# Two places in a planned attention phase: when head outputs are added up, and where memory rows' squares are written

## The chip, the cores and the metric

The kernel runs on one core of one Trainium2 chip. The metric is the device time of one execution in microseconds, as the median of several runs. A profile of one execution stands beside it, taken by the hardware profiler. The engines are called TensorE (PE; its weight loads PEld), VectorE (DVE), ScalarE (ACT), GpSimd (POOL) and SyncE (SP); SP does no arithmetic here and issues most of the transfers.

## The reference

One layer of a hybrid encoder, in f32, with 1024 positions and a width of 1024:

```python
h = rmsnorm(x, g_mix_pre)
proj = h @ w_in                       # q, k, v of 8 "fox" heads and of 8 "chunk" heads, head size 64
y_fox = forgetting_attention(...)     # causal, with a cumulative log forget-gate bias
y_chk = chunked_relpos_attention(...) # own chunk and 8 before it, with a relative-position bias
y = concat([rmsnorm(y_fox, g_fox_out), rmsnorm(y_chk, g_chk_out)])
x = x + rmsnorm(y @ w_out, g_mix_post)
h = rmsnorm(x, g_mem_pre)
mem_n = rmsnorm(mem, g_mem_kv)        # 256 memory rows
x = x + rmsnorm(memory_cross_attention(h, mem_n, w_mq, w_mk, w_mv, w_mo), g_mem_post)
h = rmsnorm(x, g_ff_pre)
x = x + rmsnorm(square(relu(h @ w_ff1)) @ w_ff2, g_ff_post)
```

## The kernel before

All matmuls keep f32 accuracy by splitting an operand into a high part, rounded to the matmul type, and a low part that holds the rest; a product is then three matmuls (high by high, low by high, high by low: lines 174 to 176).

The program has three phases: the input projection with both attentions, the output projection and the memory attention, and the feed-forward layer. The first two are laid out by a small planner, `Flow`. It keeps a clock of its own (`flow.now`). Several streams of steps for TensorE (scores, transposes of probabilities, products with v, projections as filler, and others) are offered in an order of preference; the first whose conditions hold is taken, and the clock moves on by the step's listed cost. Everything for VectorE, ScalarE, POOL and SP (named V, S, G and D) is listed with `flow.put(engine, at, cost, call, then, level)`: from `at` on it may be taken by its engine, a lower level goes first. So the listed times decide only the order in which each engine gets its instructions. On the chip each engine works through its own list in that order, and waits at an instruction until what it reads is there and the buffer that it writes is free.

`Tokens` stand for buffers: a step or a load takes tokens and later gives them back at a listed time, and `ready(n)` asks whether n are free. The buffers themselves come from pools: "u4" (line 155) has 31 buffers of 4 KB for each partition and is used for almost everything that lives long; "wraw" has three buffers for raw weights as they are loaded; "ph" (line 582) has two, in which the transposed probabilities, high and low part, wait for their product with v. The tokens of the "ph" buffers are `free["p"]`.

How one head's probabilities go: scores on TensorE (lines 515 and 516), bias and row minimum on VectorE (519), exponential on ScalarE (528), the reciprocal of the sum on VectorE (530), scaling on POOL (531), transposes on TensorE into `ptr` (588), high part on ScalarE (597), low part on VectorE (594), the product `pv` on TensorE (638), its copy `ot` on ScalarE (647), and two stores to DRAM on SP (654 and 656).

The product leaves a head output in three parts (high and low part of v by the high part of p, and high by low). They are stored into the three planes of `od[kc][th]`, where `kc` is one of the 8 blocks of 128 output columns (0 to 3 fox, 4 to 7 chunk) and `th` one of the two halves of the positions. When the eight stores of a block and half are through, `summed` (606) lists two transfers on POOL's queue that add plane 1 and then plane 2 onto plane 0 in DRAM (line 611). Both write the same rows, so the second waits until the first has landed. Only when all four blocks of a group are added may `Outputs` read them back.

`Stock` loads the weights through the "wraw" buffers in the order of a list. In this list "norm" stands ahead of the weights of the sixth pair of heads: there `mem_norm` takes all three raw buffers for the gain and for the two blocks of memory rows, squares the rows on ScalarE (line 831; only the sum along each row is used, the squares themselves go to a tile `junkm` that nobody reads), works out the inverse root on POOL, scales the rows on VectorE and stores them to DRAM on SP. "mem", further down the list, loads them back. `WeightSums` (910) adds up blocks of the memory output weights ahead of time and starts a set when eight "u4" tokens are free.

Of the kernel before, what the change touches and what calls it, by code (L numbers as in the profile page):

```python
# [14 lines left out]
F32 = mybir.dt.float32  # L15
F32R = mybir.dt.float32r
BF16 = mybir.dt.bfloat16
AF = mybir.ActivationFunctionType
# [4 lines left out]
P = 128  # L23
S = 1024
D = 1024
# [110 lines left out]
def build(ctx, tc, nc, out, t):  # L136
    def pool(name, bufs=1, space=None, stack=ctx, **kw):
        if space is not None:
            kw["space"] = space
        return stack.enter_context(tc.tile_pool(name=name, bufs=bufs, reuse_waits="tile", **kw))  # L140
# [12 lines left out]
    def u4(name, shape, dt=F32R):  # L153

        return up.tile(list(shape), dt, tag="u4", bufs=31, name=name)
# [56 lines left out]
    md = [dr.tile([P, D], F32, name=f"md{b}") for b in range(2)]  # L212
# [4 lines left out]
    p1 = pool("p1", stack=p1s)  # L217
# [8 lines left out]
    def bias_rows(part):  # L226

        if part == 0:
# [12 lines left out]
    flow = Flow()  # L241
    free = {k: Tokens(flow, n) for k, n in
            dict(s=2, tr=2, pv=2, mm=2, sp=5, p=2, klo=4, bias=2, raw=2, w=2, ot=3, qn=2, u4=7,
                 q=4, mp=4, pt=1, xt=2, wq=0).items()}
    seen = {}

    def there(*keys):
        return all(flow.past(seen.get(k, math.inf)) for k in keys)
# [4 lines left out]
    def raw_tile(name):  # L253
        return wp.tile([P, D], F32, tag="wraw", bufs=3, name=name)
# [7 lines left out]
    class Stock:  # L262
# [88 lines left out]
        def pump(self):  # L351

            while self.to_load:
                if isinstance(self.to_load[0], str):
                    n = 3 if self.to_load[0] == "norm" else 2
                    if not free["raw"].ready(n):
                        break
                    for _ in range(n):
                        free["raw"].take()
                    (mem_norm if self.to_load.pop(0) == "norm" else mem_loads)()  # L360
                    break
                key = self.to_load[0][0]
                self.spare[key] = not free["raw"].ready()
                if self.spare[key] and not (key[0] in SPARE and free["u4"].ready(12)):
                    break
                free["u4" if self.spare[key] else "raw"].take()
                self.load()
                flow.put("D", flow.now, 0.55, lambda: None, lambda at, k=key: seen.__setitem__(("raw", k), at + 4.2))
            while self.to_split and there(("raw", self.to_split[0])):
                key = self.to_split[0]  # L370
                home = self.home.get(key, "w")
                n = 1 + (home == "u4")
                if not free[home].ready(n):
                    break
                for _ in range(n):
                    free[home].take()
                self.to_split.pop(0)
                vec = key[0] not in "qkv" and (key[0] != "mk" or key[1] % 2)
                self.turned += 1

                def halves(at, key=key, eng="V" if vec else "G"):
                    e = nc.vector if eng == "V" else nc.gpsimd
                    last = lambda end: (seen.__setitem__(key, end), free["u4" if self.spare.get(key) else "raw"].give(end))
                    if eng == "V":
                        flow.put(eng, at, 1.22, lambda: self.lo(key, e), last, 1)
                    else:
                        flow.put(eng, at, 1.3, lambda: self.lo(key, e, 0), lambda end: flow.put(
                            eng, end, 1.3, lambda: self.lo(key, e, 1), last, 2), 2)

                flow.put("S", flow.now, 1.06, lambda key=key: self.hi(key), halves, 2)  # L390
# [212 lines left out]
    def value_steps():  # L603
        landed = [[all_of(("od", g, th), 4) for th in range(2)] for g in range(2)]

        def summed(kc, th):
            def add(at, m=1):
                if m == 3:
                    return landed[kc // 4][th](at)
                o = od[kc][th]  # L610
                flow.put("G", at, 0.9, lambda: nc.gpsimd.dma_start(o[0], o[m], accum_op=ALU.add, max_dma_last_dim=2048),
                         lambda end: add(end + 6.0, m + 1), 1)
            return all_of(("ot", kc, th), 8, add)

        sums = {(kc, th): summed(kc, th) for kc in range(KC) for th in range(2)}
        for n, a, g in units:
            kind, pr = ORDER[n]
# [50 lines left out]
    def all_of(key, m, then=None):  # L668

        count = [m, 0.0]  # L670

        def one(at):
            count[0] -= 1
            count[1] = max(count[1], at)
            if count[0] == 0:
                seen[key] = count[1]
                if then:
                    then(count[1])
        return one
# [139 lines left out]

    def mem_norm():  # L820

        g = raw_tile("g_mem_kv")
        nc.sync.dma_start(g, t["g_mem_kv"].to_broadcast([P, D]))
        for b in range(2):
            xt = raw_tile(f"mem{b}")
            nc.sync.dma_start(xt, t["mem"][b * P:(b + 1) * P, :])
            r, ss = (small.tile([P, 1], F32, tag=k, bufs=8, name=f"{k}_mem{b}") for k in ("rstd", "ss"))

            def square(xt=xt, ss=ss, b=b):
                junk = p1.tile([P, D], BF16, tag="ph", bufs=2, name=f"junkm{b}")  # L830
                nc.scalar.activation(junk, xt, AF.Square, scale=1.0 / 32.0, accum_out=ss)

            def root(r=r, ss=ss):
                nc.gpsimd.tensor_scalar(r, ss, EPS, None, op0=ALU.add)
                nc.gpsimd.tensor_tensor(r, r, mhalf[:, 0:1], op=ALU.pow)

            scale = lambda xt=xt, r=r: nc.vector.scalar_tensor_tensor(xt, xt, r, g, op0=ALU.mult, op1=ALU.mult)
            store = lambda xt=xt, b=b: nc.sync.dma_start(md[b], xt)
            flow.chain(flow.now + 6 + b, [("S", 1.1, square), ("G", 2.0, root), ("V", 1.3, scale), ("D", 0.55, store)],
                       lambda at, b=b: [free["raw"].give(at) for _ in range(1 + b)] and seen.__setitem__(("md", b), at))  # L840

    mem_in = []

# [673 lines left out]
    with tc.manual_schedule():  # L1517
# [96 lines left out]
        def value_banks(g, th):  # L1614
            tags = (("mm", "s"), ("tr", "pv"))[g]
            n = 264 if g == 0 else 256
            return [mm_tile([P, n], f"v{g}{th}{b}", tags[b // 2]) for b in range(4)]
# [25 lines left out]
        V = value_banks(0, 0)  # L1643
# [28 lines left out]
        V = value_banks(0, 1)  # L1672
# [38 lines left out]
    y, ss = ys["m", 1]  # L1711
# [220 lines left out]
    add = {}  # L1932
# [163 lines left out]
    with manual:  # L2096
        sums = lambda: None
        for j in range(NP):
# [10 lines left out]
            if j < AHEAD:  # L2109
                p1, g11 = saved.pop(j)  # L2110
                x = bank(f"px{j}")
            else:
                x, _, g11, add = first_row(j, w["a"])
# [250 lines left out]
```

## Time and profile before

| | us |
|---|---|
| median of 3 runs (lowest, highest) | 1458.66 (1458.56, 1458.72) |
| the profiled execution | 1458.23 |
| its span, from the first to the last instruction | 1456.4 |
| granted TensorE clock, mean | 0.999 of full speed |
| busy in the span: TensorE, VectorE, ScalarE, POOL | 1443.7, 955.3, 810.0, 409.2 |

In a row of the timeline the columns are start, duration, engine, line, operation, output and inputs, shapes, how many, and in brackets the idle time of the engine before it, with what ended it. A row of the chain has start, duration, and the engine and line that the chain goes through. "128x512" and the like are partitions by elements. Matmuls overlap: the next begins before the modelled end of the one before.

### The profile page before, as it was taken

What the parts mean: (1) busy time and instruction counts of PE and PEld (TensorE: products, weight loads), DVE (VectorE), ACT (ScalarE), POOL (GpSimd) and SP (SyncE); (2) the same over time, 40 slices, a digit from 0 to 9 for tenths busy, and PEclk for the clock granted to TensorE, in tenths of its full rate; (3) what the DMA queues carried; (4) which work ended last, traced back from release to release, by engine and by line L of the source; (5) the groups of instructions that cost most, each with busy time, mean ns of one, the idle gap of its engine ahead of it and who ended that gap; (6) DMA issues with size and microseconds to landing.
All of it is one profiled execution on the core that took longest, in us unless ns stands there. A gap on an engine that the chain in (4) does not pass through costs nothing.

```text
span 1456.4 us, 20947 instructions
## 1 busy us (share of the span) xinstructions
PE 1443.7 (99%) x7252; PEld 1221.4 (84%) x7252; DVE 955.3 (66%) x1647; ACT 810.0 (56%) x1435; POOL 409.2 (28%) x488
## 2 busy tenths in 40 slices
PE   9999999999999999999999999999999999999998
PEld 9988888788889888888888888888888888888886
DVE  4577777767667636965784697665555656655576
ACT  7457776567577654555654455545555453444442
POOL 1345566354344202421041514343331000000021
PEclk9999999999999999999999999999999999999999
DMA  8233566945538676541460646754444775345565
GB/s 334 67 100 98 139 170 173 294 111 127 135 91 250 186 230 238 176 172 59 140 222 30 211 147 235 261 195 159 159 158 160 289 311 190 136 149 190 187 246 202
DMA packets 100826, 259.44 MB, mean 178 GB/s; under 512 B 12504, under 2 KB 24928, under 8 KB 100720
## 3 DMA queue, kind: packets, MB, share of 16 engines
q1 hardware_dynamic: 95968, 249.71, 50.5%
q0 software_dynamic: 4608, 8.39, 4.0%
q8 instruction: 57, 0.93, 0.3%
q14 instruction: 49, 0.40, 0.1%
q10 hardware_dynamic: 144, 0.00, 0.0%
HBM read 181.98 MB, written 76.08 MB: 177 GB/s over the span
## 4 chain that ended last, share of the span: by engine, by line
PE 96%; DMA 1%; ACT 1%; DVE 1%; issue 0%; POOL 0%; SPq 0%; DVEq 0%; POOLq 0%; ACTq 0%
PE pv L638 4%; PE fx L175 4%; PE fx L174 4%; PE fx L176 4%; PE ptr L588 4%; PE px L176 3%; PE fy L174 3%; PE px L175 3%; PE fy L175 3%; PE px L174 3%; PE fy L176 3%; PE mq L174 2%; PE mq L176 2%; PE pz L176 2%; PE pz L175 2%; PE mq L175 2%
## 5 line engine op out<-in xcount | busy, mean ns | idle before, releaser
L594 DVE TENSOR_TENSOR p<-ptr,p 128x512 fp32r<-128x512 f32 (+1 forms) x152 | 92.2, 616 | 31.7 <-ACT p L597 30.9
L2087 ACT ACTIVATE whif<-ra 128x1024 fp32r<-128x1024 f32 x37 | 39.3, 1062 | 125.3 <-PE fy L175 62.6
L2089 DVE TENSOR_TENSOR wlof<-ra,whif 128x1024 fp32r<-128x1024 f32 x37 | 45.3, 1225 | 87.9 <-ACT whif L2087 87.9
L597 ACT ACTIVATE p<-ptr 128x512 fp32r<-128x512 f32 (+1 forms) x152 | 79.7, 538 | 38.8 <-PE ptr L588 38.2
L2201 POOL TENSOR_SCALAR rf<-sf 128x1 f32<-128x1 f32 x8 | 8.2, 1030 | 325.0 <-ACT jf L2186 324.7
L638 PE MATMUL pv<-p,vs 128*128 128x512 f32 (+1 forms) x304 | 86.5, 373 | 0.9 <-DVE p L594 0.9
L176 PE MATMUL fx<-vhif,wlof 128*128 128x512 f32 x168 | 65.4, 389 | 0.0
L174 PE MATMUL fx<-vhif,whif 128*128 128x512 f32 x168 | 65.4, 389 | 0.0
L175 PE MATMUL fx<-vlof,whif 128*128 128x512 f32 x168 | 65.4, 389 | 0.0
L1976 POOL TENSOR_TENSOR sc<-wf,wf 128x512 f32<-128x512 f32 x14 | 22.6, 1614 | 142.2 <-DMA wf<-in_w_ff 117.8
L638 PEld LDWEIGHTS pv<-p,vs 128*128 128x128 f32 x304 | 53.5, 189 | 10.2 <-DVE p L594 1.5
L174 PE MATMUL k<-hT_hi,whik 128*128 128x512 f32 x128 | 52.6, 411 | 0.0
L174 PE MATMUL mq<-h2T_hi,whimq 128*128 128x512 f32 x128 | 51.6, 403 | 0.2 <-DVE ym L1372 0.2
L647 ACT ACTIVATE ot<-pv 128x512 f32<-128x512 f32 x64 | 37.9, 593 | 24.9 <-PE pv L638 24.6
L174 PE MATMUL q<-hT_hi,whiq 128*128 128x512 f32 x128 | 51.0, 398 | 0.0
L174 PE MATMUL yw<-whiwo,yT_hi 128*128 128x512 f32 x128 | 50.8, 396 | 0.1
L175 PE MATMUL k<-hT_lo,whik 128*128 128x512 f32 x128 | 50.2, 392 | 0.0
L176 PE MATMUL k<-hT_hi,wlok 128*128 128x512 f32 x128 | 50.2, 392 | 0.0
L176 PE MATMUL q<-hT_hi,wloq 128*128 128x512 f32 x128 | 50.1, 391 | 0.0
L175 PE MATMUL q<-hT_lo,whiq 128*128 128x512 f32 x128 | 50.1, 391 | 0.0
L176 PE MATMUL mq<-h2T_hi,wlomq 128*128 128x512 f32 x128 | 50.0, 391 | 0.0
L175 PE MATMUL mq<-h2T_lo,whimq 128*128 128x512 f32 x128 | 50.0, 391 | 0.0
(670 smaller groups left out, 4953.8 us busy)
## 6 DMA issues: line engine op xcount, KB each, us to landing
ra<-gd SPq DMA_DIRECT2D x56, 512.0 KB, 3.5
wg<-in_w_ff SPq DMA_DIRECT2D x56, 512.0 KB, 4.5
wf<-in_w_ff SPq DMA_DIRECT2D x38, 512.0 KB, 3.7
gd<-s SPq DMA_DIRECT2D x48, 256.0 KB, 2.1
od<-ot SPq DMA_DIRECT2D x64, 128.0 KB, 3.1
od<-od POOLq DMA_DIRECT2D x32, 256.0 KB, 4.9
wrawmq<-in_w_mq SPq DMA_DIRECT2D x16, 512.0 KB, 4.4
gd<-u SPq DMA_DIRECT2D x32, 256.0 KB, 2.0
```

The costliest lines, as they stand in the source:

```text
L174: nc.tensor.matmul(ps, lh, rh, start=start, stop=False, skip_group_check=more)
L175: nc.tensor.matmul(ps, lh, rl, start=False, stop=False, skip_group_check=more)
L176: nc.tensor.matmul(ps, ll, rh, start=False, stop=stop, skip_group_check=more)
L588: nc.tensor.transpose(tr[:, m, :], sp[:, k * P:(k + 1) * P], ident)
L594: flow.put("V", at, 0.56 if dead else 0.7, lambda: nc.vector.tensor_sub(pl[:, live, :], tr[:, live, :], f(ph[:, live, :])), done)
L597: flow.put("S", flow.end, 0.49 if dead else 0.6, lambda ph=ph, tr=tr, live=live: nc.scalar.activation(ph[:, live, :], tr[:, live, :], AF.C ...
L638: nc.tensor.matmul(pv[:, :, q0 * P:(q0 + k1 - k0) * P], v, x[:, :, k0:k1, :].rearrange("p m k q -> p m (k q)"), start=c == 0 and m == 0, s ...
L647: nc.scalar.activation(box["t"][:, :, :, ::step], pv.rearrange("p m (k q) -> p m k q", q=P), AF.Copy)
L1976: eng.tensor_sub(sc[:, k1], r0[:, k0], r1[:, k0])
L2087: nc.scalar.activation(ah, ra, AF.Copy)
L2089: nc.vector.tensor_sub(al, ra, f(ah))
L2201: nc.gpsimd.tensor_scalar(r, ssf[b][:, 0:1], ssf[b][:, 1:2], EPS, op0=ALU.add, op1=ALU.add)
```

## The change

The two adding transfers of a block are listed later for the blocks 0 to 5: the first 3 us further behind the stores, and the next step 9 us instead of 6 us behind the end of each. Blocks 6 and 7 stay as they were. The squares of the memory rows go into a "u4" buffer, as f32, instead of a "ph" buffer, as bf16. For that `mem_norm` starts only when two "u4" tokens are free and takes both; each is given back when its square is through. The squares are listed 8 and 9 us after the loads instead of 6 and 7, and the rest of each row's chain follows its square as before.

```diff
--- before.py
+++ after.py
@@ -353,7 +353,7 @@
             while self.to_load:
                 if isinstance(self.to_load[0], str):
                     n = 3 if self.to_load[0] == "norm" else 2
-                    if not free["raw"].ready(n):
+                    if not free["raw"].ready(n) or n == 3 and not free["u4"].ready(2):
                         break
                     for _ in range(n):
                         free["raw"].take()
@@ -609,8 +609,8 @@
                     return landed[kc // 4][th](at)
                 o = od[kc][th]
                 flow.put("G", at, 0.9, lambda: nc.gpsimd.dma_start(o[0], o[m], accum_op=ALU.add, max_dma_last_dim=2048),
-                         lambda end: add(end + 6.0, m + 1), 1)
-            return all_of(("ot", kc, th), 8, add)
+                         lambda end: add(end + (6.0 if kc > 5 else 9.0), m + 1), 1)
+            return all_of(("ot", kc, th), 8, lambda at: add(at + (0.0 if kc > 5 else 3.0)))
 
         sums = {(kc, th): summed(kc, th) for kc in range(KC) for th in range(2)}
         for n, a, g in units:
@@ -819,6 +819,8 @@
 
     def mem_norm():
 
+        for _ in range(2):
+            free["u4"].take()
         g = raw_tile("g_mem_kv")
         nc.sync.dma_start(g, t["g_mem_kv"].to_broadcast([P, D]))
         for b in range(2):
@@ -827,8 +829,7 @@
             r, ss = (small.tile([P, 1], F32, tag=k, bufs=8, name=f"{k}_mem{b}") for k in ("rstd", "ss"))
 
             def square(xt=xt, ss=ss, b=b):
-                junk = p1.tile([P, D], BF16, tag="ph", bufs=2, name=f"junkm{b}")
-                nc.scalar.activation(junk, xt, AF.Square, scale=1.0 / 32.0, accum_out=ss)
+                nc.scalar.activation(u4(f"junkm{b}", (P, D), F32), xt, AF.Square, scale=1.0 / 32.0, accum_out=ss)
 
             def root(r=r, ss=ss):
                 nc.gpsimd.tensor_scalar(r, ss, EPS, None, op0=ALU.add)
@@ -836,8 +837,10 @@
 
             scale = lambda xt=xt, r=r: nc.vector.scalar_tensor_tensor(xt, xt, r, g, op0=ALU.mult, op1=ALU.mult)
             store = lambda xt=xt, b=b: nc.sync.dma_start(md[b], xt)
-            flow.chain(flow.now + 6 + b, [("S", 1.1, square), ("G", 2.0, root), ("V", 1.3, scale), ("D", 0.55, store)],
-                       lambda at, b=b: [free["raw"].give(at) for _ in range(1 + b)] and seen.__setitem__(("md", b), at))
+            rest = [("G", 2.0, root), ("V", 1.3, scale), ("D", 0.55, store)]
+            end = lambda at, b=b: [free["raw"].give(at) for _ in range(1 + b)] and seen.__setitem__(("md", b), at)
+            flow.chain(flow.now + 8 + b, [("S", 1.1, square)],
+                       lambda at, rest=rest, end=end: (free["u4"].give(at), flow.chain(at, rest, end)))
 
     mem_in = []
```

## The prediction

> **What bounds the kernel now.** I read the page first, to see which engine fills the span.
>
> ```profile
> span 1456.4 us, 20947 instructions
> PE 1443.7 (99%) x7252; PEld 1221.4 (84%) x7252; DVE 955.3 (66%) x1647; ACT 810.0 (56%) x1435; POOL 409.2 (28%) x488
> ```
>
> TensorE works 1443.7 us of 1456.4, so 12.7 us is all that anybody can win without taking matmuls away, and the change takes none away. The profiled execution itself took 1458.23 us, 1.83 more than its span; the median of the timed runs, 1458.66, is 0.43 above it. I work in differences and subtract them from the median. A measurement of this kernel tells about 0.2%, here 2.92 us, from no change.
>
> The second view is busy time by stage, to see where in the attention phase, which the change edits, TensorE rests. The columns are the stretch, its length, and each engine's busy time with its instructions (PE first, POOL fifth).
>
> ```profile
> 80.00:240.00 160.00, 160.00 (x864) 135.49 (x863) 123.22 (x330) 113.07 (x232) 90.76 (x133) 1.00 0.53 135
> 240.00:260.00 20.00, 19.14 (x106) 15.98 (x105) 14.57 (x39) 12.77 (x28) 10.37 (x20) 1.00 0.50 139
> 260.00:280.00 20.00, 20.00 (x109) 16.94 (x108) 16.44 (x31) 13.69 (x28) 6.87 (x10) 1.00 0.96 301
> 280.00:300.00 20.00, 18.23 (x98) 15.38 (x97) 12.14 (x44) 11.56 (x27) 13.16 (x16) 1.00 0.88 234
> 300.00:440.00 140.00, 140.00 (x773) 120.26 (x772) 95.46 (x255) 91.81 (x194) 57.82 (x78) 1.00 0.47 114
> 440.00:460.00 20.00, 19.62 (x141) 18.34 (x140) 13.69 (x36) 13.39 (x27) 9.97 (x11) 1.00 0.95 265
> 460.00:560.00 100.00, 99.90 (x548) 86.52 (x547) 56.87 (x110) 65.57 (x115) 19.89 (x21) 1.00 0.70 231
> ```
>
> In 480 us there are four idle spots: 0.86 us in 240 to 260, 1.77 in 280 to 300, 0.38 in 440 to 460 and 0.10 after it, 3.11 in all. The granted clock is 1.00 in each stretch, so nothing is to be had there. The third view, TensorE's own waits, names who ended the two large ones.
>
> ```profile
> PE ptr L588 <- POOL spc0g L531: 1.8, 1, 1.8
> PE pv L638 <- DVE p L594: 0.9, 1, 0.9
> ```
>
> **The memory rows' squares.** The timelines of TensorE and ScalarE, and the chain of waits between them, show how the 0.86 us comes about.
>
> ```profile
> 254.38 0.39 PE L175 MATMUL k<-hT_lo,whik 128*128 128x512 f32 x1
> 254.60 0.39 PE L176 MATMUL k<-hT_hi,wlok 128*128 128x512 f32 x1
> 255.85 0.50 PE L638 MATMUL pv<-p,vs 128*128 128x512 f32 x1 [0.86 <-DVE p L594]
> ...
> 245.25 1.06 ACT L831 ACTIVATE junkm<-mem 128x1024 bf16<-128x1024 f32 x1 [0.73 <-PE pv L638]
> 250.18 1.06 ACT L831 ACTIVATE junkm<-mem 128x1024 bf16<-128x1024 f32 x1 [2.77 <-PE pv L638]
> 253.67 0.47 ACT L597 ACTIVATE p<-ptr 128x384 fp32r<-128x384 f32 x1
> ...
> 250.18 0.81 ACT junkm L831
> 251.34 1.03 ACT spf7g L528 x2
> 252.73 1.94 POOL spf7g L531
> 255.34 0.47 DVE p L594
> ```
>
> The result of the square, which nobody reads, goes into one of the two "ph" buffers, in which turned probabilities wait for their `pv` product. So ScalarE stood for 0.73 and 2.77 us until a `pv` product had read its buffer, and the exponentials and the copy at 253.67 queued behind it. Matmuls of 512 columns start 0.22 us apart (254.38, 254.60), and the next one began 1.25 us after 254.60: TensorE lost 1.03 us, a little more than the idle time shown, because the modelled ends overlap the next start.
>
> With a buffer of the "u4" pool the two squares need no `pv` product. They stay two instructions; now their result is f32 instead of bf16, and the nearest row says that this costs nothing:
>
> ```profile
> L2087 ACT ACTIVATE whif<-ra 128x1024 fp32r<-128x1024 f32 x37 | 39.3, 1062 | 125.3 <-PE fy L175 62.6
> ```
>
> That is 1062 ns for a four-byte result of the same size, beside 1060 here. From below zero, ScalarE is freed of up to 3.5 us of standing (0.73 + 2.77); of that only the 1.03 us reached TensorE, so I take a gain of 1.03, with 0 and 1.2 as its ends.
>
> The squares are listed 2 us later, and with them the root (POOL), the scaling (VectorE) and the store (SP), and so the release of the three raw buffers, from which the next weight loads start. What hides that:
>
> ```profile
> 264.68 2.54 POOL L332 TENSOR_TENSOR wloq<-wrawq,whiq 128x512 fp32r<-128x512 f32 x2 [1.50 <-ACT whiq L323]
> 275.68 0.40 PE L174 MATMUL q<-hT_hi,whiq 128*128 128x512 f32 x1
> 254.80 0.45 SPq L942 DMA_DIRECT2D wm<-in_w_mo  x1
> ```
>
> The first weights loaded behind the rows are split at 267.22 and multiplied from 275.68, so 8.46 us lie between; two are taken, and in the trace the squares themselves should end earlier, not later. Without that cover TensorE would lose the 2 us. The two tokens of "u4" are held for some ten listed microseconds. The next taker in that stretch is the second set of weight sums, whose loads begin at 254.80 and which the code starts only with eight tokens free; so the pool had eight to spare, and the new condition on two does not hold the rows back. If the two came back late, these sums would slip, and they are read much later. I cost both at nothing.
>
> **The adding transfers.** The 1.77 us, by the timelines of TensorE and POOL, the reciprocal on VectorE, the chain, and the answer for the adding line:
>
> ```profile
> 289.82 0.39 PE L176 MATMUL q<-hT_hi,wloq 128*128 128x512 f32 x1
> 291.98 0.33 PE L588 MATMUL ptr<-ident,spc0g 128*128 128x128 f32 x1 [1.77 <-POOL spc0g L531]
> ...
> 279.70 0.15 POOL L460 MEMSET biasc<- 64x64 f32 x1 [7.87 <-DMA biasc<-rd]
> 283.55 0.92 POOL L611 DMA_DIRECT2D od<-od  x1 [0.74 <-DMA kd<-kd]
> 287.02 0.36 POOL L531 TENSOR_SCALAR spc0g<-spc0g,smc0g 128x128 f32<-128x128 f32 x1 [2.55 <-DVE smc0g L530]
> 290.55 0.85 POOL L611 DMA_DIRECT2D od<-od  x1 [3.17 <-DMA od<-od]
> 291.17 0.76 POOL L531 TENSOR_SCALAR spc0g<-spc0g,smc0g 128x256 f32<-128x256 f32 x1
> ...
> 287.58 0.16 DVE L530 RECIPROCAL smc0g<-smc0g 128x1 f32<-128x1 f32 x1
> ...
> 283.55 6.61 DMA od<-od
> ...
> L611 POOL DMA_DIRECT2D od<-od x32: 807/846/1111, 136.6 to 512.7; - x32
> ...
>   DMA od<-od: 25.1, 6
> ...
> DMA to landing us min/median/max: 3.9/4.9/9.0
> ```
>
> POOL works in list order. The first add went at 283.55; the second, on the same rows, had to wait for it to land (6.61 us) and stood in POOL's queue from 287.38 to 290.55. The scaling of 128x256 probabilities, ready at 287.74 when its reciprocal ended, stood behind it, and `ptr` on TensorE behind that. TensorE should have gone on at 290.04 (289.82 + 0.22) and went on at 291.98: 1.94 us lost. The plan sets the second add 6 us behind the end of the first (0.9 us); POOL reached the first late, after 7.87 us of waiting for a bias row, and so came to the second 3.83 us after the first instead of 6.9.
>
> With the change the spacing is 9 for the output columns 0 to 5. By the same lateness POOL comes to the second add 6.83 us after the first; the first has landed and let go after 7.00 (290.55 less 283.55). A wait of 0.17 us is left, and the scaling has room: ready at 287.74 and 0.76 long, it was not needed until 290.04, 1.54 us of slack. Besides, the second add stands about 6 us further back (3 behind the stores, 3 behind the first), so this scaling should come out ahead of it. I take the whole 1.94 as gained. The bounds: a landing of 9.0 us gives a wait of 2.56 and, less 1.54, a loss of 1.0, a gain of 0.9; the upper end is 1.94. The other waits for a landing (25.1 us in six, this one included) did not reach TensorE, and their going gains nothing. Each of the moved adds, 6 columns by 2 halves by 2, still issues once, at 0.846 us of POOL; none is added. The last two columns, on which the output projection waits, keep their spacing.
>
> The Trainium skill, "DMA: Bandwidth & Descriptors", section "Anatomy of one DMA — SWDGE (gpsimd) path", gives a transfer issued by GpSimd about 2.0 us plus its bytes over 436 GB/s; as an estimate from that page these 256 KB land after 2.6 us, and then the old spacing of 6 would have left time over and the wider one would buy nothing. The trace does not agree: 3.9 at the least, 4.9 in the middle, 6.61 at this place.
>
> **The sum.** 1.03 + 1.94 = 2.97 us; 1458.66 - 2.97 = 1455.7. In the profiled execution the span would go to 1453.4. What is late next is nothing that the stages 80 to 240 and 300 to 440 show, where TensorE never rests.
>
> **The rivals.** *First, the second wait stays* (the adds' lateness on POOL grows with the spacing, or landings get as long as 9.0): only the squares gain, 1458.66 - 1.03 = 1457.6. For it: POOL already lost 3.1 us of the listed 6.9. Against: the wait is 0.17 by the same lateness.
>
> *Second, slower: the moved adds come to stand directly ahead of scalings that TensorE waits for.* The place is POOL's list from the first add (136.6) on; the list is worked out anew from there, and every scaling behind it may change places with an add. The price is 0.846 us an add. With 2.97 gained, four such adds (3.4) turn the sign, and 2.97 + 2.92 = 5.9, seven of the 24, make it slower by over 0.2%: with eight, 1458.66 - 2.97 + 6.8 = 1462.5. For it: the row at 291.98 shows TensorE taking a scaling straight from POOL, and the new order can't be read off the old trace. Against: POOL is busy 57.82 of 140 us in 300 to 440, and of 32 adds one reached TensorE.
>
> *Third, more goes than I count*: with the idle spots of 440 to 560 (0.38 and 0.10) and another 0.4 from small waits, 2.97 + 0.9 = 3.87, 1454.8. *Fourth, nothing moves*: the "u4" pool or POOL's order puts the same standing in another place, 1458.7.
>
> **How the numbers follow.** The forecast, both waits gone, gets 0.52. Its own range is 1454.7 to 1457.0, and since 2.97 stands just beyond the bound of 2.92 and a small new wait in the re-made order is easily had, I put 0.38 of it beyond the bound and 0.14 within. First rival 0.16, within. Second 0.22: 0.20 slower, 0.02 within. Third 0.06, faster. Fourth 0.04, within. So faster 0.38 + 0.06 = 0.44; within 0.14 + 0.16 + 0.02 + 0.04 = 0.36; slower 0.20. The range goes from the third rival, 1454.7, to 1461.5, where the second starts to count as slower; that leaves out its 0.20 at the most.
>
> **What would show it.** Right: ScalarE's wait for `pv` ahead of the squares gone and no TensorE wait for `p` near 255; in 280 to 300 TensorE at 20.00; no wait `ptr` behind a scaling of `spc0g`; the adding line's wait for itself well under 25.1 us. Wrong: TensorE waits of over 0.3 us at new places between 137 and 500, above all behind POOL's scalings with an add just ahead; or `pv` waiting for ScalarE behind squares that now stand for a "u4" buffer.

## The result, and the profile after

The changed kernel took 1455.92 us (median of 19 runs) and the kernel before 1458.76 beside it, a ratio of 0.9981 (95% interval 0.9975 to 0.9988): 2.84 us or 0.19% less, just inside the 0.2% that the prediction set as its bound of "no change". In a second set of runs it was 1456.04 against 1457.95, again 0.9981 (0.9970 to 0.9993). The ratios given here and below are those on record; they can differ a little from the quotient of the two medians, which is 0.9987 in this second set. The profile shown here is that of the second set (1456.04 us), since the execution profiled in the first took 3764.3 us; that one is counted in the median and left out of the ratio.

The page: the span, and each engine's busy time.

```profile
span 1454.3 us, 20942 instructions
PE 1444.9 (99%) x7252; PEld 1222.5 (84%) x7252; DVE 962.6 (66%) x1647; ACT 809.4 (56%) x1435; POOL 408.6 (28%) x488
```

The span is 2.1 us shorter. Busy time by stage, in the columns of before:

```profile
240.00:260.00 20.00, 20.00 (x113) 16.87 (x112) 15.39 (x44) 14.54 (x31) 11.31 (x22) 1.00 0.59 146
260.00:280.00 20.00, 20.00 (x107) 16.87 (x106) 17.13 (x27) 12.61 (x25) 10.24 (x10) 1.00 0.96 315
280.00:300.00 20.00, 20.00 (x109) 17.17 (x108) 14.51 (x49) 13.66 (x32) 11.43 (x18) 1.00 0.83 225
440.00:460.00 20.00, 19.56 (x143) 18.43 (x142) 13.40 (x40) 13.55 (x28) 10.46 (x11) 1.00 0.93 280
```

The two idle spots that the prediction priced are filled: 19.14 and 18.23 us of 20 are now 20.00 and 20.00. TensorE's waits (us in total, times, longest) no longer name `ptr` behind `spc0g`, nor `pv` behind `p`. The first row below is a new wait, in the feed-forward phase; the second stood in the kernel before as well, at the same size:

```profile
PE pz L174 <- DVE g L2142: 0.6, 1, 0.6
PE sc6g L515 <- DVE mnc6g L519: 0.4, 1, 0.4
```

The timelines of ScalarE and POOL at the two places:

```profile
249.81 1.05 ACT L832 ACTIVATE junkm<-mem 128x1024 f32<-128x1024 f32 x1
253.53 1.06 ACT L832 ACTIVATE junkm<-mem 128x1024 f32<-128x1024 f32 x1
...
274.89 0.14 POOL L460 MEMSET biasc<- 64x64 f32 x1 [1.38 <-DMA biasc<-rd]
280.15 0.92 POOL L611 DMA_DIRECT2D od<-od  x1 [0.95 <-DMA od<-ot]
285.60 0.36 POOL L531 TENSOR_SCALAR spc0g<-spc0g,smc0g 128x128 f32<-128x128 f32 x1 [4.54 <-DVE smc0g L530]
286.56 0.48 POOL L531 TENSOR_SCALAR spc0g<-spc0g,smc0g 128x256 f32<-128x256 f32 x1 [0.60 <-DVE smc0g L530]
288.07 1.26 POOL L531 TENSOR_SCALAR spc0g<-spc0g,smc0g 128x384 f32<-128x384 f32 x2 [1.02 <-DVE smc0g L530]
291.12 0.85 POOL L611 DMA_DIRECT2D od<-od  x1 [1.79 <-DMA od<-ot]
```

The squares wait for nothing, and the f32 result costs what the bf16 one did. The scaling of 128x256 stands ahead of the next add and waits only for its reciprocal. The row to keep for later is the one at 274.89: the bias row is there 4.81 us earlier than before (279.70), and POOL, which now has two splits of weights to do just ahead of it, waited 1.38 us for it instead of 7.87. The adding line's own waits halved, from 25.1 us in six to 13.0 in three, while the landings themselves kept their 4.9 us median:

```profile
  DMA od<-od: 13.0, 3
...
DMA to landing us min/median/max: 4.0/4.9/7.9
```

How the gain runs through the program is read off the first matmul of three phases, in us behind the first gate transposes (58.72 us into the span before, 58.60 after): the memory scores start 2.89 us earlier (561.03, now 558.14), the first `pz` product of the feed-forward layer 2.85 earlier (822.30, now 819.45), but its last `fx` product only 1.78 (1390.78, now 1389.00). So the attention phase gave the 2.97 us of the sum to within 0.1, and 1.1 of it was given back far behind the change.

### The profile page after: what moved, and what is told of

Same layout as the page of the kernel before. It is cut to its first block, busy times and chain, and to the rows that moved or that the text cites. A ratio compares the mean times of both kernels' runs of the same rounds, so it can differ in the third digit from the quotient of the medians.

```text
span 3762.5 us, 20942 instructions
## 1 busy us (share of the span) xinstructions
PE 3755.2 (100%) x7252; PEld 2388.7 (63%) x7252; DVE 963.5 (26%) x1647; ACT 827.0 (22%) x1435; POOL 380.6 (10%) x488
## 4 chain that ended last, share of the span: by engine, by line
PE 100%; DVE 0%; DVEq 0%; POOLq 0%; ACT 0%; issue 0%; POOL 0%; ACTq 0%
PE pv L638 4%; PE ptr L588 4%; PE fx L174 4%; PE fx L175 4%; PE fx L176 4%; PE px L176 3%; PE px L174 3%; PE fy L176 3%; PE fy L174 3%; PE fy L175 3%; PE px L175 3%; PE yw L174 2%; PE k L176 2%; PE k L175 2%; PE mq L175 2%; PE yw L175 2%
## 5 line engine op out<-in xcount | busy, mean ns | idle before, releaser
L638 PE MATMUL pv<-p,vs 128*128 128x512 f32 (+1 forms) x304 | 196.2, 772 | 0.0
L175 PE MATMUL fx<-vlof,whif 128*128 128x512 f32 x168 | 139.4, 830 | 0.0
L174 PE MATMUL fx<-vhif,whif 128*128 128x512 f32 x168 | 139.4, 830 | 0.0
L176 PE MATMUL fx<-vhif,wlof 128*128 128x512 f32 x168 | 139.1, 828 | 0.0
L174 PE MATMUL k<-hT_hi,whik 128*128 128x512 f32 x128 | 110.4, 863 | 0.0
L174 PE MATMUL mq<-h2T_hi,whimq 128*128 128x512 f32 x128 | 109.2, 853 | 0.0
L176 PE MATMUL fy<-vhif,wlof 128*128 128x512 f32 x128 | 106.1, 829 | 0.0
L175 PE MATMUL yw<-wlowo,yT_hi 128*128 128x512 f32 x128 | 106.0, 828 | 0.0
L176 PE MATMUL yw<-whiwo,yT_lo 128*128 128x512 f32 x128 | 106.0, 828 | 0.0
L174 PE MATMUL fy<-vhif,whif 128*128 128x512 f32 x128 | 105.7, 826 | 0.0
```

Of the source, the lines that this page charges most:

```text
L174: nc.tensor.matmul(ps, lh, rh, start=start, stop=False, skip_group_check=more)
L175: nc.tensor.matmul(ps, lh, rl, start=False, stop=False, skip_group_check=more)
L176: nc.tensor.matmul(ps, ll, rh, start=False, stop=stop, skip_group_check=more)
L638: nc.tensor.matmul(pv[:, :, q0 * P:(q0 + k1 - k0) * P], v, x[:, :, k0:k1, :].rearrange("p m k q -> p m (k q)"), start=c == 0 and m == 0, s ...
```

## The experiments

Ratios are to the kernel before on the same chip; its medians in the three sets were 1457.95, 1458.35 and 1458.24 us. The three sets ran on three chips, and no kernel but the one before ran in more than one of them, so small differences between parts of different sets say little. Each profile is of one execution, and its time is given where it lies far from the median. Two readings were put against each other: that the two waits are two, each removed by its own edit (the prediction), and that they are one chain that begins at the squares.

**The changed kernel again**, to have a whole profile beside the parts:

> The changed kernel once more, for a profile. Theory (two TensorE waits go, 1.03 and 1.94 us, and nothing new comes): span 1453.4, 2.8 to 3.0 us below before, TensorE idle in the attention phase at most 0.6 us. Rival (more of the gain comes from a re-made order of all steps, with waits elsewhere gone and others new): the two waits gone, but other waits of over 0.3 us at new places, and the sum agrees with 2.8 only by chance.

1456.04 us, 0.9981 (0.9970 to 0.9993), as shown above. The two waits are gone and TensorE rests 0.52 us between 80 and 560, as the theory had it; the span is 1454.3 instead of 1453.4, and the new wait of 0.6 us lies far behind, at 968.

**Only the adds' edit** (both numbers; the squares as before):

```diff
-                         lambda end: add(end + 6.0, m + 1), 1)
-            return all_of(("ot", kc, th), 8, add)
+                         lambda end: add(end + (6.0 if kc > 5 else 9.0), m + 1), 1)
+            return all_of(("ot", kc, th), 8, lambda at: add(at + (0.0 if kc > 5 else 3.0)))
```

> Only the adding transfers are listed later and further apart; squares as before. Theory: the wait behind the scaling of spc0g goes (1.94 us), the wait for p near 255 stays (1.03): 1.9 us below before. Rival (one edit carries all): 0 or 2.8 below.

1456.32 us, 0.9986 (0.9978 to 0.9995). Both waits are gone, the one for `p` near 255 too, which this edit was not thought to touch: the engines' orders came out anew, and in this order the squares stood for a "ph" buffer for 0.19 us in all instead of 3.50. So about the expected gain came, but not by the expected way: two waits went, and in place of the two TensorE waits once at 448.7:

```profile
PE mk L174 <- DVE km_lo L869: 1.7, 1, 1.7
```

**Only the squares' edit**, listed 8 and 9 us behind the loads as in the change:

```diff
-                junk = p1.tile([P, D], BF16, tag="ph", bufs=2, name=f"junkm{b}")
-                nc.scalar.activation(junk, xt, AF.Square, scale=1.0 / 32.0, accum_out=ss)
+                nc.scalar.activation(u4(f"junkm{b}", (P, D), F32), xt, AF.Square, scale=1.0 / 32.0, accum_out=ss)
...
-            flow.chain(flow.now + 6 + b, [("S", 1.1, square), ("G", 2.0, root), ("V", 1.3, scale), ("D", 0.55, store)],
+            flow.chain(flow.now + 8 + b, [("S", 1.1, square)],
```

> Only the squares go into the large pool, listed 2 us later; adds as before. Theory: the wait for p near 255 goes (1.03 us), the wait behind the scaling of spc0g stays within 0.3 of 1.94: 1.0 us below before. Rival: the re-made order moves the second wait too, so that the gain is not 1.0.

1458.50 us, 0.9998 (0.9989 to 1.0007): no gain, where 1.0 us was expected. The wait near 255 is gone, and three others stand in its place. The largest, on TensorE's timeline, and the row on ScalarE that causes it:

```profile
269.83 0.66 PE L783 MATMUL vtr<-ident,vt 128*128 128x128 f32 x4 [1.16 <-DVE p L594]
...
266.53 1.06 ACT L323 ACTIVATE whiq<-wrawq 128x1024 fp32r<-128x1024 f32 x1 [2.76 <-DMA wrawq<-in_w_qk]
```

The rounding of the next head's weights stands in ScalarE's queue 2.76 us for its load, with an exponential, a copy and the high parts of two turned blocks behind it. The load takes a raw buffer that the memory rows give back, and the rows are now done later: their first store goes out at 256.28 instead of 254.21, and the load at 259.97 instead of 258.16. In the kernel before the same row is:

```profile
263.54 1.05 ACT L323 ACTIVATE whiq<-wrawq 128x1024 fp32r<-128x1024 f32 x1
```

By the starts of its matmuls TensorE lost 1.33 us at 268.3, and 0.53 and 0.75 at 291.0 and 298.3.

**The squares' edit, but listed 6 and 7 us behind the loads as before** (`flow.now + 6 + b` in the last line of the diff above):

> The squares go into the large pool with their tokens, but stay listed 6 and 7 us behind the loads; adds as before. Theory (the buffer, not the listed time, made the wait): the wait for p near 255 goes as well, 1.0 us below before. Rival (the listed time counts, because the rows land late): ScalarE waits for the rows' landing instead of a pv product, 0.5 us or more of it reaches TensorE, and the gain is under 0.5.

1456.09 us, 0.9983 (0.9975 to 0.9992). Both waits are gone, with not one number of the adds' listing changed, and with every engine's instructions in the order of before. The memory scores start 3.05 us earlier (561.03, now 557.98 us behind the gate transposes), where 1.0 was expected.

**Only the buffer**: the squares in "u4", still bf16, no tokens, listed as before. Every engine has exactly the instructions of the kernel before in the same order; one buffer is another.

```diff
-                junk = p1.tile([P, D], BF16, tag="ph", bufs=2, name=f"junkm{b}")
+                junk = u4(f"junkm{b}", (P, D), BF16)
```

> The kernel before, with the squares written into a buffer of the large pool and nothing else: no tokens, no listed time, no adding transfer changed, and every engine's order is that of before. Theory A (the two waits are one: ScalarE's standing for a pv product makes VectorE's scaling, SP's stores and so the bias row late, POOL comes late to the first add, and the second add then waits): both TensorE waits go, the one behind the scaling of spc0g to under 0.3 us, 2.6 to 3.0 us below before. Theory B (two waits that have nothing to do with each other, as the prediction has it): only 1.03 gained, the wait behind the scaling stays at 1.5 or more.

1455.88 us, 0.9985 (0.9976 to 0.9993). Of the two waits neither is left. By that ratio 2.2 us are gained, where 2.6 to 3.0 were expected for one chain and 1.03 for two; the interval, 1.0 to 3.5, does not exclude the 1.03, so it is the waits that tell the two readings apart. The timeline of POOL in this run:

```profile
275.95 0.15 POOL L460 MEMSET biasc<- 64x64 f32 x1 [5.82 <-DMA biasc<-rd]
...
279.53 0.91 POOL L611 DMA_DIRECT2D od<-od  x1
285.82 0.36 POOL L531 TENSOR_SCALAR spc0g<-spc0g,smc0g 128x128 f32<-128x128 f32 x1 [5.38 <-DMA kd<-kd]
286.41 0.85 POOL L611 DMA_DIRECT2D od<-od  x1 [0.23 <-issue]
287.02 0.76 POOL L531 TENSOR_SCALAR spc0g<-spc0g,smc0g 128x256 f32<-128x256 f32 x1
```

The adds are listed where they were, the second still stands ahead of the scaling, and it no longer waits for the first: the first went at 279.53 instead of 283.55. Where the four microseconds come from is seen on ScalarE, VectorE and SP. First the kernel before, then the run with the buffer alone:

```profile
252.27 0.58 ACT L647 ACTIVATE ot<-pv 128x512 f32<-128x512 f32 x1
252.48 1.29 DVE L837 SCALAR_TENSOR_TENSOR mem<-mem,rstd_mem,g_mem_kv 128x1024 f32<-128x1024 f32 x1
...
252.87 0.60 SPq L654 DMA_DIRECT2D od<-ot  x1
253.52 0.60 SPq L656 DMA_DIRECT2D od<-ot  x1
254.21 0.54 SPq L838 DMA_DIRECT2D md<-mem  x1
258.16 0.33 SPq L310 DMA_DIRECT2D wrawq<-in_w_qk  x1
272.87 0.54 SPq L456 DMA_DIRECT2D biasc<-rd  x1
```

```profile
249.62 0.60 ACT L647 ACTIVATE ot<-pv 128x512 f32<-128x512 f32 x1 [0.56 <-PE pv L638]
250.22 1.27 DVE L837 SCALAR_TENSOR_TENSOR mem<-mem,rstd_mem,g_mem_kv 128x1024 f32<-128x1024 f32 x1
...
250.25 0.60 SPq L654 DMA_DIRECT2D od<-ot  x1
250.90 0.60 SPq L656 DMA_DIRECT2D od<-ot  x1
251.59 0.54 SPq L838 DMA_DIRECT2D md<-mem  x1
255.04 0.33 SPq L310 DMA_DIRECT2D wrawq<-in_w_qk  x1
269.37 0.54 SPq L456 DMA_DIRECT2D biasc<-rd  x1
```

In the kernel before, the exponential `spf7g` and the copy `ot` of a head output stood behind the second square in ScalarE's queue; the square began at 250.18, and at 246.42 with the buffer. So the copy came 2.65 us later than in the run with the buffer (252.27, 249.62). The head of SP's queue waited for that copy to store it: its store goes out 2.62 us later (252.87, 250.25), and what stands behind it in the queue is as late, the store of the first memory rows (254.21, 251.59) by 2.62, the load into the raw buffer that these rows free (258.16, 255.04) by 3.12, and the bias row (272.87, 269.37) by 3.50. VectorE's scaling of the memory rows was late by 2.26 as well (252.48, 250.22), since the reciprocal ahead of it waited 1.61 us for the same exponential. But it ended at 253.77, and the rows' store went out at 254.21, directly behind the two stores of the head output; so in the kernel before it was the copy on ScalarE that set SP's time.

So with the buffer POOL begins on the bias row 3.75 us earlier (279.70, 275.95) and reaches the first add 4.02 earlier, while TensorE reaches the scores of `sc0g` only 1.20 earlier. That is how the second add's wait for a landing went, and TensorE is at 20.00 of 20 us in 280 to 300 here too.

TensorE reaches the `sc1g` scores, which come behind both places, 2.67 us earlier than before (239.75, now 237.08 us behind the gate transposes). The profiled execution is the slowest of the 11, which lie between 1455.60 and 1458.26: TensorE lost 2.40 us in it at another place, at 449.8 (the wait was 0.4 before and is 0.4 with the whole change).

```profile
PE sc6g L515 <- DVE mnc6g L519: 2.2, 1, 2.2
```

**The one add left out**, of block 3 and its second half, in the kernel before:

```diff
-                flow.put("G", at, 0.9, lambda: nc.gpsimd.dma_start(o[0], o[m], accum_op=ALU.add, max_dma_last_dim=2048),
+                flow.put("G", at, 0.9, lambda: (kc, th, m) == (3, 1, 2) or nc.gpsimd.dma_start(o[0], o[m], accum_op=ALU.add, max_dma_last_dim=2048),
```

> The kernel before, without the second adding transfer of block 3, second half (one plane of the sum is left out); all else in the same order. Theory (the TensorE wait at 291.98 is that transfer's wait for the landing of the first): this wait goes, 1.9 us below before, and the wait for p near 255 stays at 1.03. Rival (POOL's lateness makes the wait, whatever stands in its queue): the scaling is still late by over 1 us, and less than 1 is gained.

1458.69 us, 1.0001 (0.9992 to 1.0010). The stage and the other wait:

```profile
280.00:300.00 20.00, 19.84 (x105) 16.73 (x104) 14.65 (x47) 12.71 (x30) 13.41 (x16) 1.00 0.79 220
...
PE pv L638 <- DVE p L594: 0.9, 1, 0.9
```

The second wait went down to 0.2 us, the first stayed: taken from this end the chain is cut behind its beginning. The 1.9 us that were expected did not come. Of the 1.61 us by which the `sc1g` scores come earlier (239.75, now 238.14 us behind the gate transposes), 0.81 is left at the memory scores (561.03, 560.22) and 0.37 at the last `fx`, and in the timed runs nothing can be told from no change.

**Only the spacing of 9**, and **only the 3 us behind the stores**:

```diff
-                         lambda end: add(end + 6.0, m + 1), 1)
+                         lambda end: add(end + (6.0 if kc > 5 else 9.0), m + 1), 1)
```

> The kernel before, with only the 9 us instead of 6 between the adding transfers of blocks 0 to 5, not listed further behind the stores; squares as before. Theory (the spacing opens the wait): the wait behind the scaling goes, 1.9 below before, the wait for p near 255 stays. Rival (what counts is the re-made order behind it): waits at other places than these two, by over 0.5 us in all, and a gain that is not 1.9.

```diff
-            return all_of(("ot", kc, th), 8, add)
+            return all_of(("ot", kc, th), 8, lambda at: add(at + (0.0 if kc > 5 else 3.0)))
```

> The kernel before, with only the first adding transfers of blocks 0 to 5 listed 3 us further behind the stores, spacing 6 as before; squares as before. Theory (the spacing counts, not the delay): the second add stands as long behind the first as before, the wait behind the scaling stays within 0.5 of 1.94. Rival (the re-made order counts): that wait goes or halves, and others come.

The spacing alone is slower: 1461.12 us, 1.0020 (1.0011 to 1.0029). The 3 us alone: 1457.65, 0.9995 (0.9985 to 1.0006); in that profile (1456.72 us, the second fastest of 11) both waits are gone, and the squares stand for 1.25 us once. So neither theory came true. In the run with the 3 us POOL still waited 7.10 us for the bias row and came to the first add only at 286.62; but five scalings of `spc0g` stand between it and the next add (295.21), and no `ptr` waits. With the spacing alone (profile of 1463.92 us, the slowest of its 11), the wait behind the scaling was still 1.0 us (at 294.84), and TensorE waited for another transfer; the granted clock of the stage fell behind that pause, and the profile puts the wait of POOL's second add down to that transfer as well:

```profile
PE sc0g L516 <- DMA kl<-kl: 3.1, 1, 3.1
...
280.00:300.00 20.00, 15.92 (x69) 12.97 (x68) 7.75 (x27) 8.16 (x18) 10.37 (x13) 0.83 0.82 198
...
293.40 0.86 POOL L611 DMA_DIRECT2D od<-od  x1 [6.52 <-DMA kl<-kl]
```

That copy of keys was issued at 285.35 and landed after 7.13 us, with the first add's transfer (issued at 282.57) under way. Whether the add held it up is not settled; no run separates them.

**The whole change with the squares listed early**, **only the late listing** (squares in "ph", `flow.now + 8 + b`), **the buffer with the 3 us**, and **the buffer with the adds' edit** (the last two with the bf16 buffer, no tokens, listed as before):

> The whole change, but with the squares listed where they were listed before (6 and 7 us behind the loads instead of 8 and 9). With the squares' edit alone the early listing took 0.9983 of the time before and the late one 0.9998. Theory A (one chain: ScalarE's standing makes VectorE, SP's queue and the bias row late, and so POOL's adds; with it gone the adds' listing has nothing left to do): no wait for p near 255 and none behind spc0g near 292, 1455.5 to 1456.5 us, ratio 0.9980 to 0.9987, no better than the squares' edit alone with the early listing. Rival B (the two edits add up, as the prediction had it): 1.9 us below the squares' edit alone, some 1454.2 us, ratio under 0.9975. Rival C (the late listing is what makes the adds' edit safe): a new wait behind spc0g or mnc0g of over 1 us and a ratio over 0.9990.

> Of the change only the 2 us by which the squares are listed later; they stay in the ph buffers, as bf16, and no u4 token is taken. Theory A (what counts is how long ScalarE stands for ph, in whatever order): if the re-made order lets the squares stand for 0.5 us or more each, the waits for p near 255 and behind spc0g near 292 are both there, 1457.5 to 1459 us, ratio 0.9995 to 1.0008; if it does not, both are gone together, ratio 0.9980 to 0.9990. Rival (the late listing is what hurts the squares' edit alone): the three waits of that run, for p at 268 and 298 and behind spc0g at 291, show here too, at about the same size, ratio at or over 0.9998. One of the two large waits going without the other speaks for two separate waits.

> Squares in u4 buffers (as bf16, no tokens, listed where they were) and the adds 3 us further behind the stores, spacing 6. Every engine's order is that of the run with the 3 us alone (0.9995, in whose profile both large waits were gone and ScalarE stood 1.2 us for ph once). Theory A: the buffer takes 1.2 us of standing that reached nothing, so the time is that of the 3 us alone within 0.6 us, ratio 0.9980 to 1.0000, waits as there. Rival (the buffer by itself is worth about 2 us, by some other way than the chain): ratio under 0.9980, 2 us below the run with the 3 us alone.

> Both edits of the adds, and the squares in u4 buffers (as bf16, no tokens, listed where they were). Every engine's order is that of the run with the adds' edits alone (0.9986; ScalarE stood 0.2 us for ph there; TensorE lost 1.9 us to a wait of mk for km_lo at 449). Theory A: nothing is left for the buffer to take away in this order, 1455.7 to 1456.9 us, ratio 0.9980 to 0.9990, the wait at 449 as likely as there. Rival B (the two edits add up): 1 us or more below the adds' edits alone, some 1455.2 us, ratio under 0.9979.

Only the late listing: 1460.03 us, 1.0011 (1.0002 to 1.0020), with the three waits of the squares' edit alone. The profile is of a slower execution (1461.87 us; six of the 11 are at or under 1460.03), and the first of the waits is larger in it:

```profile
270.78 1.11 PE L783 MATMUL vtr<-ident,vt 128*128 128x128 f32 x4 [2.25 <-DVE p L594]
...
267.48 1.06 ACT L323 ACTIVATE whiq<-wrawq 128x1024 fp32r<-128x1024 f32 x1 [3.85 <-DMA wrawq<-in_w_qk]
```

So it is the late listing that spoils the squares' edit by itself, as the rival of that expectation had it, and the buffer gives some 0.13% in that order too (1.0011 less 0.9998; the intervals overlap between 1.0002 and 1.0007 and the two ran on different chips, so its size is rough). Theory A of that expectation failed: the squares stood 1.78 us in two goes, and neither large wait came at its old place and size.

The whole change listed early was expected at 0.9980 to 0.9987 and missed: 1457.33 us, 0.9993 (0.9984 to 1.0002). Both waits are gone. In the profile, which is of the slowest execution (1459.34), TensorE loses 2.21 us at 449 to the wait of `mk` for `km_lo` that the adds' edit alone had, and more behind it at a lower clock (last section). The buffer with the 3 us: 1457.56, 0.9993 (0.9984 to 1.0002), beside 0.9995 for the 3 us alone. The buffer with the adds' edit: 1457.37, 0.9992 (0.9983 to 1.0001), just outside the 0.9980 to 0.9990 expected, beside 0.9986 for the adds' edit alone. In neither does the buffer add a gain once the order spares the squares most of their standing, and Rival B, with both edits' gains in one run, is outside the intervals of both; the edits do not add up. The grid of them, ratios to the kernel before:

| squares | adds as before | adds as changed |
|---|---|---|
| "ph", listed 6 | 1 | 0.9986 |
| "u4" bf16, no tokens, listed 6 | 0.9985 | 0.9992 |
| "u4" f32, tokens, listed 6 | 0.9983 | 0.9993 |
| "u4" f32, tokens, listed 8 | 0.9998 | 0.9981 |
| "ph", listed 8 | 1.0011 | not run |

Each ratio has an interval of about 0.0009 to each side, so 0.9981 to 0.9986 are not told apart, and none of the parts beats the whole change.

The traces say more about this grid: the order of every engine's instructions goes with the listed times alone, whatever the buffer, its type and the tokens. So the three rows listed at 6 share one order in each column, the two listed at 8 in the first column share another, and within these only the buffers differ. In the two orders in which the squares stood long in "ph" (3.50 us in the order of before, 1.78 listed at 8) the other buffer takes 0.13 to 0.17% away; in the two in which they stood 0.19 (the adds' edit) and 1.25 (the 3 us alone) no gain is seen. The three runs of one order in the last column, 0.9986 to 0.9993, lie within each other's intervals.

## Why the prediction was right, and where not

**The result and what would show it: right.** The time lies 0.2 us above the forecast, though just within the bound of "no change", beyond which the prediction had put most of this case's chance. The signs named for it are there: no standing ahead of the squares, no wait for `p` near 255, 20.00 in 280 to 300, no `ptr` behind a scaling of `spc0g`, 13.0 us of the adding line's waits for itself, and no new TensorE wait of over 0.3 us between 137 and 500. "This scaling should come out ahead" of the second add held as well (286.56, with the next add at 291.12). That the f32 squares and the tokens cost nothing is borne out by the squares' rows.

**The sum, 1.03 + 1.94: right in size, in part by luck, and wrong in what it adds.** The prediction gave each wait to its own edit and costed the gain of the squares' edit at 1.03, "of that only the 1.03 us reached TensorE". In the order of before the buffer alone, with no instruction moved, removes both (0.9985, and 0.9983 as f32 and with tokens). The standing reached TensorE twice: once through `p`, and some 35 us later through the copy that stood behind the squares on ScalarE, the stores on SP that waited for it, the bias row behind them and POOL. The prediction saw the last link ("POOL reached the first late, after 7.87 us of waiting for a bias row") and took that lateness as given, "by the same lateness", when it worked out the wider spacing. Followed back along SP's queue, to what had held the bias row's issue, it would have led to the squares. The total came out because the change holds the edit that takes both waits away; for that edit alone the prediction's sum would have given 1.03. How the gain of the whole change divides is not shown: its order is one of its own, and the kernel of that order with the squares in "ph" was not run.

**The spacing's term: not shown to be worth anything by itself.** The spacing alone is slower (1.0020), the 3 us alone make no difference that can be told (0.9995), and both together gain (0.9986) with the squares still in "ph", in an order in which the squares hardly stand (0.19 us). What the prediction said besides, that with the adds further back the scaling comes out ahead, is seen in the run with the 3 us alone: there POOL was as late as ever for the bias row and no `ptr` waited. That the whole of 1.94 us is had by the spacing is not what happened.

**"I cost both at nothing": half wrong.** For the squares listed 2 us later, the cover named was the 8.46 us between POOL's split of the next weights and their use. The step behind the load that comes due first is another: ScalarE's rounding of the same weights (the prediction's own row at 264.68 names it as what POOL waited for), which waits in its queue with exponentials behind it. In the squares' edit alone it stood 2.76 us and TensorE lost 1.33; that, with the two smaller waits, ate the gain. In the whole change the rounding comes out later (269.01, with no wait), so the price did not fall due; the prediction gave no ground to expect that.

**The rivals.** The slower case, adds directly ahead of scalings, did not come. The one slower version of the adds, the spacing alone, was slower through a transfer of keys. "A small new wait in the re-made order is easily had" did come, at 968 instead of between 137 and 500: TensorE lost 0.78 us there, the larger part of what was given back. The last section shows what it is.

## What to carry to other kernels

When a wait comes from an instruction that was reached late, follow the lateness back through the in-order queues to the instruction that first stood, before pricing a remedy at the place where it shows; two idle spots 35 us apart were one chain here, and the cheapest cure was at its head: a result that nobody reads had been put into a scarce buffer. Cover for a moved load must be looked for at each of its readers, and the first to queue for it counts, not the last. Where a planner makes the order anew, parts tried one by one do not add up, so try the whole as well as the parts, and look whether each part's new waits come from its mechanism or from the order. Where two kernels turn out to have the same order, their difference is that of the one thing left.

## What the runs showed of the hardware

The give-back in the feed-forward phase is a meeting of two engines. The timelines of VectorE and POOL there, first before, then after:

```profile
963.42 1.24 DVE L2168 TENSOR_TENSOR s<-u,g 128x512 f32<-128x512 f32 x1
964.69 0.69 DVE L2170 TENSOR_TENSOR u<-p1r,u 128x512 f32<-128x512 f32 x1
...
962.81 1.30 POOL L1983 TENSOR_TENSOR sd<-wf,sc 128x512 f32<-128x512 f32 x1
```

```profile
962.02 1.67 DVE L2173 TENSOR_TENSOR u<-p1r,u 128x512 f32<-128x512 f32 x1
...
961.52 1.63 POOL L1986 TENSOR_TENSOR sd<-wf,sc 128x512 f32<-128x512 f32 x1
```

The same instruction, `u<-p1r,u` (the edit moves its line from 2170 to 2173), takes 0.69 us when it starts 1.88 us behind POOL's, and 1.67 when it starts 0.50 behind it: then it ends at 963.69, 0.54 after POOL's (963.15), as if it had stood until that was through. Over the thirteen profiles used here there are only these two: in seven it starts 1.88 us behind and takes 0.69, in six (the whole change, the early squares, the buffer, the 3 us, the buffer with the 3 us, the late listing) it starts 0.50 behind and takes 1.66 to 1.67. The `g` that the `pz` product waits for ends 5.62 us behind its start in the seven and 6.59 to 6.61 in the six. TensorE loses 0.55 to 1.00 us there in five of the six, and in none of the seven.

The instruction ahead of it, `s<-u,g`, meets an instruction of POOL in all thirteen (1.24 us in the kernel before). In these nineteen meetings VectorE's instruction begins 0.06 to 1.03 us behind POOL's, takes 0.81 to 1.79, and ends 0.55 us behind the end of POOL's each time, so its length is set by POOL's end. The price comes with the moment at which the phase meets POOL's work, and not with one of the edits: POOL's four instructions begin 77.5 to 78.2 us behind the first `pz` product in the seven and 78.8 to 79.7 in the six, and the phase has the same instructions in all.

The Trainium skill, "SBUF — State Buffer", section "SBUF: two separate sides", says that VectorE, in an instruction with two inputs in SBUF, and a GpSimd instruction that reads SBUF share a pair of ports under an exclusive lock, and that the later of the two blocks until the other is done. The nineteen meetings agree with that. The wait at 449 with the adds' edit has such a meeting on its way: two `kl` instructions take 3.12 us from 447.07, beside POOL's two from 446.65, and 1.40 us in the whole change, where they run from 444.51, ahead of POOL's. How much of that wait it makes was not tried.

Some pauses cost more than their length. Busy time in stretches of 5 us, granted clock in the last column but two: the whole change listed early, and the late listing, each behind a pause of TensorE (2.21 us at 449.2, 2.42 at 268.1 by the starts of the matmuls); then the buffer alone behind a pause of 2.40 us at 449.8:

```profile
450.00:455.00 5.00, 3.43 (x18) 3.43 (x19) 4.02 (x4) 1.28 (x3) 4.78 (x4) 0.73 0.83 151
455.00:460.00 5.00, 5.00 (x38) 4.91 (x37) 3.36 (x17) 3.60 (x10) 1.72 (x4) 0.93 1.00 392
```

```profile
271.00:276.00 5.00, 5.00 (x22) 4.15 (x22) 4.22 (x6) 2.09 (x4) 1.71 (x4) 0.68 0.89 253
```

```profile
455.00:460.00 5.00, 5.00 (x42) 4.96 (x41) 4.08 (x18) 4.54 (x11) 2.59 (x5) 1.00 1.02 311
```

By the first two, 27% of 5 us and 7% of the next are 1.7 us lost beside the pause of 2.21; from the first `sc4g` score to the last of `sc7g` that kernel took 92.47 us and the whole change, whose order is another, 88.17, 4.3 more; the adds' edit alone, in the same order and with a pause of 1.88 us at 448.7 that left the clock at 1.00, took 90.66. The third row, 32% of 5 us, is 1.6 us beside 2.42. Behind the pause of the buffer alone the clock stayed at 1.00, so the length of a pause does not decide it by itself. The Trainium skill, "TensorE: Matmul & The Clock Gate", section "What's actually happening", has the clock set by activity in windows of some 3.4 us that run on regardless of the kernel, and by that a pause can fall within one window or across two; it names an idle window of that length as what lowers the clock, and here pauses of 2.2 and 2.4 us were enough.

The transfers of 256 KB that add in DRAM took 3.9 to 10.0 us to land in these profiles, with medians between 4.7 and 5.1, whatever their spacing; what went with the change is the standing for them, not their length.
